# New durations in a list scheduler: the pace of products, and VectorE and GpSimd waiting for each other

## The chip, the cores and the metric

The kernel runs as one program on one core of a Trainium2 chip. The metric is the device time of one execution in microseconds. Before the change it is 1493.85 us, the median of three runs (1490.75 to 1494.23).

Engines are named as in the profile: PE is TensorE, DVE is VectorE, ACT is ScalarE, POOL is GpSimd, and SP is the engine that issues most of the DMAs.

## The reference

256 tokens of 1024 features, with 16 learned meta tokens ahead of them, go through two blocks of two layers each. All is fp32, and each layer is a mixer and a feed-forward part, with norms and residual adds around them:

```python
def first_block(x, meta_tokens, norm_w, ...):        # the meta tokens stand ahead of x
    for i in range(DEPTH):                           # DEPTH = 2
        a_in = rms_norm(hs, norm_w[i, 0])
        mix = gated_deltanet(a_in, ...) if i == 0 else mlstm(a_in, ...)
        hs = hs + keep * rms_norm(mix, norm_w[i, 1])
        f = conv_ffn(rms_norm(hs, norm_w[i, 2]), ...)
        hs = hs + keep * rms_norm(f, norm_w[i, 3])
```

The mixer of the first layer, where most of the kernel's waits lie, is the gated delta rule, in chunks. For each head it needs decay matrices, the products of keys with keys, the inverse of a triangular matrix made from these, and a state that goes from chunk to chunk:

```python
    decay = jnp.exp(jnp.where(incl, G[..., :, None] - G[..., None, :], -jnp.inf))
    a_mat = jnp.eye(CHUNK) + jnp.einsum('bhnid,bhnjd->bhnij', kb, kc) * decay * strict
    sol = lax.linalg.triangular_solve(a_mat, rhs, left_side=True, lower=True)
    ...
    o = rms_norm(o, norm_w) * jax.nn.silu(z)
    return o.reshape(B, L, GDN_VAL_DIM) @ w_out
```

The second block has an even layer (short convolution and sliding-window attention) and an odd layer (gated linear attention and latent attention), each with a SwiGLU feed-forward part. Its mixers and feed-forward parts end in `hs = layer_norm(ALPHA * hs + f)`, where the mean and the variance are taken over the features of a token.

## The kernel before

**Products.** Activations are feature-major: 128 features on the partitions, tokens along the free axis (272 with the meta tokens in the first block, 256 in the second). The weights are streamed once, in 413 chunks of eight tiles of 128 x 128 (`wload`). For each chunk ACT writes the rounded part `wh` (L326) and DVE the remainder `wl` (L327). Each fp32 product is then three matmuls on such parts: `wh` with the high part of the activation, `wh` with its low part, `wl` with its high part (`mm3`, L350 to L352; the same three in `group`, L373, L374 and L376, which works on several products side by side).

**The first mixer** (`gdn`) works in four groups of four heads. A string lists the stages of the groups: projections q, v and z, blocks P, inverses D, token-major values and keys T, states S and outputs O. The parts that matter here:

- Decay matrices, once for all groups: DVE multiplies a mask by the gates (L713, tile `gl_`), PE sums it (L717), ACT takes the exponential (L271) and POOL masks the result (L719, tile `E`).
- Each projection goes through a convolution over tokens: ACT scales, DVE adds three shifted products (L727, tile `kq` or `v`). For the first two projections of group 0 the source is `v_first` in SBUF, otherwise PSUM.
- `gdn_blocks`: products of keys with keys (L810 and L819), then the diagonal blocks of 16 are inverted by substitution on POOL: 15 pairs of a product (L840) and a subtraction (L842), 30 steps. After that POOL takes a power (L843).
- `gdn_inverse`: the inverse is doubled from 16 to 128 by a chain of small products on PE with copies on DVE and ACT between them (L882 is the first, L888 the second).
- `gdn_out`: each output chunk `o` gets its norm: DVE makes the mean square `ss` (L1060 for chunks of 128 tokens), POOL its power (L1064), DVE scales `o` (L1067), PE transposes (L1068), DVE multiplies by the gate (L1071).

The norms of the first block's residuals are made in `post_norm` (a power on POOL at L555).

**The second block's stages** end in `layer_norm`. It works on eight feature tiles m: PE's product, DVE's residual add (L1255 for m < 4, L1259 above), the mean taken out of later and earlier tiles (L1269, L1271), ACT's square, running sums on POOL (L1257, L1263 for the values, L1249 for the squares). Ahead of the last tile's statistics PE sums over the features (`stat_cols`, L422). Where a stage follows, `not_normed` writes high and low parts of the values before the norm is known (ACT L1241, DVE L1242), and PE begins the next stage's products on them (`group`).

**What sets the order.** The kernel is traced as a plain program. Then `IssueOrder` puts each engine's instructions in the order of its queue. It knows the dependencies that the tiles imply, a duration for each instruction (`cost`), the time from the end of an instruction to the start of one on another engine that waits for it (the table HOPS, in `lag`), and a model of TensorE's clock. `search` runs list schedules forwards and backwards in turn, three rounds: `forward` gives starts, `backward` gives due times from the end, and the next `forward` takes the most urgent instruction that is ready. `fix` then writes the order that it finds into the program, as dependencies that need no semaphore. Nothing else follows from the durations: not the instructions, nor their tiles.

Of the kernel before, what the change touches and what calls it, by code (L numbers as in the profile page):

```python
# [13 lines left out]
D = 1024  # L14
# [18 lines left out]
# ---------------------------------------------------------------- host layout  # L33
# [40 lines left out]
# the order of the first mixer: projections q (with k), v and z, products and blocks P, inverses D, token-major values and keys T, states S, outputs O  # L74
# [65 lines left out]
def host(inp):  # L140
# [34 lines left out]
    # second block, even layer: head t of kv 0 beside head 4 + t of kv 1  # L175
# [10 lines left out]
    # odd layer  # L186
# [56 lines left out]
    n = -(-w.shape[0] // CH)  # L243
# [15 lines left out]
# ---------------------------------------------------------------- device  # L259
class Kern:  # L260
# [8 lines left out]
    # ---- helpers  # L269
# [40 lines left out]
    def wload(self, first, need, ahead):  # L310
        """Chunks of weights up to `need`, and `ahead` more as far as the buffers behind `first` go."""
# [27 lines left out]
    def wrow(self):  # L339
        """The next four parts side by side."""  # L340
        ci, j = divmod(self.wpos, CH)
        assert j + 4 <= CH
        for _ in range(4):
            self.wnext()
        return [a[:, j:j + 4].rearrange("p a b -> p (a b)") for a in self.wchunks[ci]]
# [16 lines left out]
    def group(self, items, hook=None):  # L362
        """Several products of K = 8 side by side, so that each part of x serves all of them as it comes."""
# [19 lines left out]
    def halves(self, x, n):  # L383
        """The first four products of K = 16: the last part of x is taken last."""
# [23 lines left out]
    def warm(self, k, ins=None):  # L408
        """Products that nothing reads, behind `ins`, so that the array's clock stays up over a wait."""
# [9 lines left out]
    def stat_cols(self, st, src, n):  # L419
        """Sums over the partitions, one column for each 128 tokens (the last ones overlap)."""  # L420
        for i, s in enumerate(starts(n)):
            r = self.nc.tensor.matmul(st[:, i:i + 1], src[:, s:s + 128], self.ones1, start=True, stop=True)  # L422
        return r

    def bcast(self, out, col, n):
        """A column for each 128 tokens to rows on all partitions."""
# [7 lines left out]
    def row_stat(self, acc, sq, n, warm=0):  # L434
        """Sum of squares over all tiles: the running sum and the last tile."""
# [6 lines left out]
    def acc_sq(self, acc, prev, sq, m):  # L442
        """Running sum of the squares of all tiles but the last."""
# [15 lines left out]
    def rstd(self, st, n, dim, pool, tag="rsy"):  # L459
        """1 / sqrt(st / dim + 1e-6), the same rows on all partitions."""  # L460
# [16 lines left out]
    # ---- norms of the first block  # L477
# [5 lines left out]
    def first_raw(self, pool):  # L483
        """The input of the first mixer, not yet normed, and the columns of its sums of squares."""
# [24 lines left out]
    def pre_norm(self, wname, t0, pool, items, outs, dest=None, st=None, tag="rsy"):  # L509
        """The first products of a stage from its input before the norm, scaled after; then the normed input."""  # L510
# [19 lines left out]
    def post_norm(self, wname, K, x, t0, pool, nxt, tag='mix'):  # L530
        """Output projection, its norm, the residual; then the input of the next stage, not yet normed."""
# [46 lines left out]
    # ---- feed-forward with convolution  # L578
# [38 lines left out]
    # ---- gated delta rule  # L617
    def gdn(self):
# [5 lines left out]
        with ExitStack() as es:  # L624
# [17 lines left out]
            # gates  # L642
# [45 lines left out]
            # cumulative sums and last values  # L688
# [13 lines left out]
            # decay matrices, [j, i]: exponents are the sums of g over j < t <= i  # L702
# [77 lines left out]
    def gdn_blocks(self, g, kq, kq16, E, beta, elg, pool, dpool):  # L780
        """Norms of k, scaled products (attention over E) and the inverses of the diagonal blocks of 16."""
# [9 lines left out]
        # the meta tokens, four heads in slots of 32  # L791
# [3 lines left out]
        # products of keys with keys; the squared norms of the keys on their diagonals  # L795
# [27 lines left out]
        # decayed  # L823
# [3 lines left out]
        # the diagonal blocks of 16, one on a partition  # L827
# [5 lines left out]
        # their inverses by substitution  # L833
# [10 lines left out]
        # products of keys with queries  # L844
# [11 lines left out]
    def gdn_inverse(self, g, X64, Uf, st, pool):  # L856
        """The inverse of the triangular matrix, transposed."""
# [6 lines left out]
        # doubling: blocks of 32, 64 and 128  # L864
# [60 lines left out]
    def gdn_tokens(self, g, kq, v, kq16, v16, st, pool):  # L925
        """Values and keys with the tokens on the partitions, scaled."""
# [29 lines left out]
    def gdn_state(self, g, kq, st, neg, egl, pool):  # L956
        """The states before each chunk; the new values of each chunk take the place of the values."""
# [48 lines left out]
    def gdn_out(self, g, kq, E, st, eg, of, pool):  # L1006
        """The outputs, normed and gated, in place of the gates."""
# [12 lines left out]
        # squared norms of q, one column for each token  # L1020
# [16 lines left out]
        for c in (2, 0, 1):  # L1037
# [16 lines left out]
            # head norm  # L1054
# [21 lines left out]
    # ---- mLSTM  # L1076
# [135 lines left out]
    # ---- second block  # L1212
# [3 lines left out]
    def layer_norm(self, name, K, x, pool, last=False, tags=("xr0", "xr1", "xr2", "xr3")):  # L1216
# [11 lines left out]
        if not last:  # L1228
            # the input of the next stage, not yet normed; beside it the gain and the offset as columns
# [82 lines left out]
    def norm_product(self, i, raw, pool, out=None, scale=1.0):  # L1312
        """A product of an input before the layer norm: without its offset, and the offset; or all of it."""
# [33 lines left out]
    def softmax(self, pool, sbank, tag, scale, mask, sink, vT, out, tp=None):  # L1347
        """sbank: scores [query, (256 keys of block 1 | 128 keys of block 0)], out: [dv, 256 queries]."""
# [81 lines left out]
    def odd(self, xf):  # L1430
# [5 lines left out]
        with tc.tile_pool(name="op", bufs=1, reuse_waits="tile") as pool:  # L1436
# [18 lines left out]
            # gates of the linear attention, rotary key, queries and keys  # L1455
# [22 lines left out]
            # linear attention: decayed products, level by level  # L1478
# [44 lines left out]
            # latent attention: queries, keys, values  # L1523
# [118 lines left out]
    # ---- whole program  # L1642
# [38 lines left out]
# ---------------------------------------------------------------- issue order  # L1681
# [3 lines left out]
# ns from the end of an instruction to the start of one on another engine (or the same) that waits for it  # L1685
# [13 lines left out]
class IssueOrder:  # L1699
    """Orders the traced instructions of each engine: list scheduling, forwards and backwards in turn, over the  # L1700
# [352 lines left out]
```

## Time and profile before

| | |
|---|---|
| time, median of three runs | 1493.85 us (1490.75 to 1494.23) |
| the profiled execution: span | 1496.2 us |
| instructions | 30607 |
| mean granted clock of PE | 0.984 |
| PE busy | 1456.1 us (97%), 12258 matmuls |
| DVE busy | 1056.8 us (71%) |
| ACT busy | 842.9 us (56%) |
| POOL busy | 188.4 us (13%) |
| DMA | 223.96 MB, 150 GB/s on average |
| chain that ended last | PE 86%, DVE 6%, DMA 2%, POOL 2%, issue 2%, ACT 1% |

The profiled execution's own time is its span, 1496.2 us; it is one execution, and 2.35 us above the median of the three timed runs. Times in the rows below are microseconds from the start of this span. A matmul's busy time overlaps with that of the next one, so its pace is read from many of them in a window, and not from the duration of one.

### The profile page before, as it was taken

The numbers are of one execution on the slowest core, as the hardware profiler recorded it, in microseconds if no ns is written. First come the engines' busy times: TensorE is split into PE (matmuls) and PEld (weight loads), VectorE is DVE, ScalarE is ACT, GpSimd is POOL, SyncE is SP. The second block draws the span as 40 slices with busy tenths as digits, with TensorE's granted clock in tenths as the row PEclk, the third lists the DMA queues.
The fourth block names the chain that finished last, engine by engine and source line by source line (L and its number), as shares of the span: only waits on it lengthen the run. The fifth ranks groups of instructions, "written<-read, shape, count | busy, mean of one in ns | idle before, by whom it ended". The sixth has DMA issues, their size and how long they took to land.

```text
span 1496.2 us, 30607 instructions
## 1 busy us (share of the span) xinstructions
PE 1456.1 (97%) x12258; PEld 1403.7 (94%) x12258; DVE 1056.8 (71%) x1976; ACT 842.9 (56%) x1560; POOL 188.4 (13%) x286
## 2 busy tenths in 40 slices
PE   8899999999999999999999999999999999999997
PEld 7898998998999989889999998999999978999997
DVE  8996585548988357657988456686556798875553
ACT  5456565546766446446766446565444666654442
POOL 3472032121000120003000000020001200300011
PEclk9999998999999999999999999989999999999999
DMA  4343422354655534323665543537555424375551
GB/s 161 103 132 103 150 81 62 112 171 147 215 171 180 172 127 157 119 78 119 206 197 179 189 155 113 176 107 222 187 182 183 144 72 155 128 220 188 182 186 57
DMA packets 72670, 223.96 MB, mean 150 GB/s; under 512 B 16784, under 2 KB 18896, under 8 KB 72400
## 3 DMA queue, kind: packets, MB, share of 16 engines
q1 hardware_dynamic: 71952, 220.38, 45.5%
q8 instruction: 96, 1.57, 0.4%
q10 hardware_dynamic: 576, 1.62, 0.3%
q14 instruction: 46, 0.38, 0.1%
HBM read 220.34 MB, written 1.64 MB: 148 GB/s over the span
## 4 chain that ended last, share of the span: by engine, by line
PE 86%; DVE 6%; DMA 2%; POOL 2%; issue 2%; ACT 1%; SPq 0%; DVEq 0%; ACTq 0%; POOLq 0%
PE acc L352 17%; PE acc L350 17%; PE acc L351 17%; PE psa L350 3%; PE psa L352 3%; PE psa L351 3%; PE psb L351 2%; PE psb L352 2%; PE psb L350 2%; PE acc L376 1%; PE acc L373 1%; PE acc L374 1%; DVE wl L327 1%; POOL Xb L842 1%; DVE hs L564 1%
## 5 line engine op out<-in xcount | busy, mean ns | idle before, releaser
L327 DVE TENSOR_TENSOR wl<-wraw,wh 128x1024 fp32r<-128x1024 f32 x413 | 508.1, 1233 | 228.2 <-ACT wh L326 226.8
L326 ACT ACTIVATE wh<-wraw 128x1024 fp32r<-128x1024 f32 x413 | 435.2, 1056 | 277.8 <-PE acc L351 154.9
L352 PE MATMUL acc<-xh,wl 128*128 128x256 f32 (+1 forms) x848 | 246.7, 291 | 1.2 <-DVE wl L327 1.2
L350 PE MATMUL acc<-xh,wh 128*128 128x256 f32 (+1 forms) x848 | 245.5, 290 | 1.0 <-DVE kq L727 1.0
L351 PE MATMUL acc<-xl,wh 128*128 128x256 f32 (+1 forms) x848 | 245.6, 290 | 0.7 <-issue 0.7
L350 PE MATMUL acc<-ah,wh 128*128 128x256 f32 (+1 forms) x704 | 198.0, 283 | 0.0
L351 PE MATMUL acc<-al,wh 128*128 128x256 f32 (+1 forms) x704 | 197.9, 282 | 0.0
L352 PE MATMUL acc<-ah,wl 128*128 128x256 f32 (+1 forms) x704 | 196.7, 282 | 0.0
L352 PEld LDWEIGHTS acc<-xh,wl 128*128 128x128 f32 x848 | 161.5, 191 | 4.3 <-issue 1.7
L350 PEld LDWEIGHTS acc<-xh,wh 128*128 128x128 f32 x848 | 161.3, 190 | 2.4 <-ACT wh L326 1.2
L351 PEld LDWEIGHTS acc<-xl,wh 128*128 128x128 f32 x848 | 161.1, 190 | 1.5 <-issue 0.9
L350 PEld LDWEIGHTS acc<-ah,wh 128*128 128x128 f32 x704 | 132.5, 189 | 0.1
L351 PEld LDWEIGHTS acc<-al,wh 128*128 128x128 f32 x704 | 132.5, 189 | 0.1
L352 PEld LDWEIGHTS acc<-ah,wl 128*128 128x128 f32 x704 | 131.9, 188 | 0.0
L352 PE MATMUL acc<-xnh,wl 128*128 128x272 f32 (+1 forms) x424 | 122.2, 288 | 0.0
L350 PE MATMUL acc<-xnh,wh 128*128 128x272 f32 (+1 forms) x424 | 122.0, 288 | 0.0
L351 PE MATMUL acc<-xnl,wh 128*128 128x272 f32 (+1 forms) x424 | 121.9, 287 | 0.0
L352 PE MATMUL acc<-oh,wl 128*128 128x256 f32 (+2 forms) x304 | 86.4, 286 | 0.5 <-DVE wl L327 0.5
L351 PE MATMUL acc<-ol,wh 128*128 128x256 f32 (+2 forms) x304 | 86.1, 285 | 0.1
L350 PE MATMUL acc<-oh,wh 128*128 128x256 f32 (+2 forms) x304 | 85.2, 286 | 0.0
L350 PEld LDWEIGHTS acc<-xnh,wh 128*128 128x128 f32 x424 | 79.8, 188 | 1.5 <-issue 1.3
L352 PEld LDWEIGHTS acc<-xnh,wl 128*128 128x128 f32 x424 | 79.8, 188 | 1.4 <-issue 1.2
(715 smaller groups left out, 3483.8 us busy)
## 6 DMA issues: line engine op xcount, KB each, us to landing
wraw<-in_w_dram SPq DMA_DIRECT2D x413, 512.0 KB, 3.4
late<-in_late_dram ACTq DMA_DIRECT2D x1, 1206.5 KB, 5.7
hs<-in_x_dram SPq DMA_DIRECT2D x4, 272.0 KB
out_dram<-hs SPq DMA_DIRECT2D x8, 128.0 KB, 1.9
d<-PT SPq DMA_DIRECT2D x32, 9.0 KB, 1.5
cst<-in_cst_dram SPq DMA_DIRECT2D x1, 339.5 KB
A<-d SPq DMA_DIRECT2D x4, 72.0 KB
d<-Xb SPq DMA_DIRECT2D x4, 72.0 KB
```

The lines of the kernel that those rows point to most:

```text
L326: nc.scalar.activation(h, raw, AF.Copy)
L327: nc.vector.tensor_tensor(l, raw, h.bitcast(F32), ALU.subtract)
L350: mm(ps, h, xh, start=start, stop=False)
L351: mm(ps, h, xl, start=False, stop=False)
L352: mm(ps, l, xh, start=False, stop=stop)
L373: mm(o, h, x(k)[0], start=k == 0, stop=False)
L374: mm(o, l, x(k)[0], start=False, stop=False)
L376: mm(o, w[k][0][:, :m], x(k)[1], start=False, stop=k == KD - 1)
L564: V.tensor_tensor(hs, hs, t, ALU.add)
L842: GP.tensor_tensor(Xb[:, j + 1:16, 0:m], Xb[:, j + 1:16, 0:m], tv, sub)
```

## The change

Two durations and one rule change in `IssueOrder`; the rest of the diff takes out comments, and is left out here.

- `cost`: a product matmul of more than 64 output rows on split parts (and a transpose) had N / 2.4 + 2.4 ns for N columns (at least for 256). It now has 0.442 N + 5.5 ns, and at least 112. At 64 output rows or fewer the old formula stays.
- `shares` is new. It marks every tensor-tensor operation and copy of POOL, and each instruction of DVE that reads more than one operand of more than one element a row from SBUF.
- `forward`: a marked instruction doesn't start before the last marked one of the other of these two engines has ended. `backward` is as it was.

```diff
         self.time, self.cols, self.lead = zip(*cost)
+        self.port = [not e and self.shares(k) for k, e in enumerate(self.edge)]
...
+    def shares(self, k):
+        i = self.ins[k]
+        if self.eng[k] == POOL:
+            return str(i.opcode) == "TensorTensor" or str(i.opcode) == "TensorCopy"
+        if self.eng[k] != DVE:
+            return False
+        big = [a for a in i.ins if hasattr(a, "bass_ap") and a.bass_ap.tensor.space != bass.MemoryType.PSUM
+               and row_size([m for _, m in a.ap]) > 1]
+        return len(big) > 1
...
             if ins[0].dtype != F32 or i.is_transpose:
-                return max(n, 256 if m > 64 else 0) / 2.4 + 2.4, n * rows / 128, lead
+                return (max(0.442 * n + 5.5, 112) if m > 64 else n / 2.4 + 2.4), n * rows / 128, lead
...
         last, ticks = -1e3, {}
+        shared, owner = 0.0, DVE
         order, start = [[] for _ in ENGINES], [0.0] * n
...
             d, k = pop(now[e])
             t = max(t, ready[k])
+            if self.port[k] and owner != e:
+                t = max(t, shared)
...
                 free[e] = end = t + self.time[k]
+            if self.port[k]:
+                shared, owner = end, e
             start[k] = t
```

What moves is best seen in the queues. The first place is DVE's queue at the decay matrices of the first mixer. `gl__382`, `gl__405`, `gl__428` and `gl__451` are the masked gates of groups 0 to 3, `v_134` is `v_first`, `kq_474` the convolved queries and keys of group 0. Before:

```order
L713 TENSOR_TENSOR gl__405<-strict_378,gg_346 128x512 x2
L327 TENSOR_TENSOR wl_278<-wraw_275,wh_277 128x1024
L713 TENSOR_TENSOR gl__405<-strict_378,gg_346 128x128
L713 TENSOR_TENSOR gl__428<-strict_378,gg_346 128x512
L727 SCALAR_TENSOR_TENSOR kq_474<-v_134,par_110,kq_474 128x271
L713 TENSOR_TENSOR gl__428<-strict_378,gg_346 128x512
L713 TENSOR_TENSOR gl__428<-strict_378,gg_346 128x128
L713 TENSOR_TENSOR gl__451<-strict_378,gg_346 128x512
L727 SCALAR_TENSOR_TENSOR kq_474<-v_134,par_110,kq_474 128x270
L713 TENSOR_TENSOR gl__451<-strict_378,gg_346 128x512
L727 SCALAR_TENSOR_TENSOR kq_474<-v_134,par_110,kq_474 128x269
L727 SCALAR_TENSOR_TENSOR kq_474<-v_134,par_110,kq_474 128x271
```

After the change, from the second `gl` of group 1 on:

```order
L713 TENSOR_TENSOR gl__405<-strict_378,gg_346 128x512
L727 SCALAR_TENSOR_TENSOR kq_474<-acc_485,par_110,kq_474 128x271
L713 TENSOR_TENSOR gl__405<-strict_378,gg_346 128x128
L696 COPY gc_362<-psb0_367 128x36
L697 TENSOR_TENSOR elg_365<-psb0_367,gc_362 128x36
L713 TENSOR_TENSOR gl__428<-strict_378,gg_346 128x512 x2
L727 SCALAR_TENSOR_TENSOR kq_474<-acc_485,par_110,kq_474 128x270
L713 TENSOR_TENSOR gl__428<-strict_378,gg_346 128x128
L713 TENSOR_TENSOR gl__451<-strict_378,gg_346 128x512 x2
L713 TENSOR_TENSOR gl__451<-strict_378,gg_346 128x128
```

Of the steps that read `v_134`, four (two of 271 elements, two of 270) now stand ahead of the first `gl`, and one of 269 just ahead of the first of these rows; the weight split `wl_278` stands ahead of the first `gl` too. Two steps that read PSUM (`acc_485`) have come in between.

The second place is POOL's queue in the blocks of the last group. L840 and L842 are the substitution steps of that group, and `ss1_3081` is the mean square of an output chunk of the group before it. The difference:

```order
 L840 TENSOR_TENSOR tt1_2832<-A161_2829,Xb1_2831 72x48
 L842 TENSOR_TENSOR Xb1_2831<-Xb1_2831,tt1_2832 72x12x4
+L1064 TENSOR_TENSOR ss1_3081<-ss1_3081,fst_81 128x4
 L840 TENSOR_TENSOR tt1_2832<-A161_2829,Xb1_2831 72x55
 L842 TENSOR_TENSOR Xb1_2831<-Xb1_2831,tt1_2832 72x11x5
@@ -166,5 +168,4 @@
 L842 TENSOR_TENSOR Xb1_2831<-Xb1_2831,tt1_2832 72x4x12
 L840 TENSOR_TENSOR tt1_2832<-A161_2829,Xb1_2831 72x39
-L1064 TENSOR_TENSOR ss1_3081<-ss1_3081,fst_81 128x4
 L842 TENSOR_TENSOR Xb1_2831<-Xb1_2831,tt1_2832 72x3x13
 L840 TENSOR_TENSOR tt1_2832<-A161_2829,Xb1_2831 72x28
```

The power stood behind the 25th substitution step and now stands behind the 8th.

The third place is DVE's queue in the layer norm behind the even layer's mixer. `acc_12152`, `acc_12190` and `acc_12234` are the products of the last three feature tiles, `xr_11948` and `xr_11949` the low parts for the next stage. Before:

```order
L1269 SCALAR_TENSOR_TENSOR hs_76<-hs_76,lnpc_11939 128x256
L1259 TENSOR_TENSOR hs_76<-hs_76,acc_12152 128x256
L1242 SCALAR_TENSOR_TENSOR xr_11948<-hs_76,late_4464,xr_11946 128x256 x4
L327 TENSOR_TENSOR wl_12238<-wraw_12235,wh_12237 128x1024
L1259 TENSOR_TENSOR hs_76<-hs_76,acc_12190 128x256
L1242 SCALAR_TENSOR_TENSOR xr_11949<-hs_76,late_4464,xr_11947 128x256 x2
L327 TENSOR_TENSOR wl_12349<-wraw_12346,wh_12348 128x1024
L1259 TENSOR_TENSOR hs_76<-hs_76,acc_12234 128x256
L1277 TENSOR_SCALAR lnp1_11941<-psb1_11940 128x2
```

After the change:

```order
L1259 TENSOR_TENSOR hs_76<-hs_76,acc_12152 128x256
L1269 SCALAR_TENSOR_TENSOR hs_76<-hs_76,lnpc_11939 128x256
L1242 SCALAR_TENSOR_TENSOR xr_11948<-hs_76,late_4464,xr_11946 128x256
L1259 TENSOR_TENSOR hs_76<-hs_76,acc_12190 128x256
L327 TENSOR_TENSOR wl_12238<-wraw_12235,wh_12237 128x1024
L1242 SCALAR_TENSOR_TENSOR xr_11948<-hs_76,late_4464,xr_11946 128x256
L1259 TENSOR_TENSOR hs_76<-hs_76,acc_12234 128x256
L1242 SCALAR_TENSOR_TENSOR xr_11948<-hs_76,late_4464,xr_11946 128x256 x2
L1277 TENSOR_SCALAR lnp1_11941<-psb1_11940 128x2
```

Three of the four low-part steps and the weight split have moved behind the residual add of `acc_12190`. On PE the sums over the features (L422) stood right behind the last matmul of `acc_12234`; eight matmuls of the next stage's `group` now stand between them.

## Rows read from the trace of the kernel before

**Rows 1.** The page's first part: busy us, share of the span, instructions.

```profile
PE 1456.1 (97%) x12258; PEld 1403.7 (94%) x12258; DVE 1056.8 (71%) x1976; ACT 842.9 (56%) x1560; POOL 188.4 (13%) x286
```

**Rows 2.** Undisturbed windows: length, busy time (and count) by engine, granted clock, DMA share, GB/s.

```profile
440.00:480.00 40.00, 40.00 (x320) 40.00 (x319) 34.07 (x59) 26.75 (x43) 0.00 (x0) 1.00 0.54 176
...
1040.00:1080.00 40.00, 40.00 (x340) 40.00 (x340) 22.46 (x28) 18.99 (x29) 0.00 (x0) 1.00 0.56 186
```

**Rows 3.** Windows with waits, the same columns (PE, PEld, DVE, ACT, POOL).

```profile
0.00:330.00 330.00, 313.96 (x3152) 295.97 (x3153) 234.97 (x535) 186.12 (x419) 99.27 (x195) 0.97 0.38 119
...
540.00:560.00 20.00, 17.27 (x134) 15.96 (x133) 14.24 (x28) 9.55 (x21) 7.22 (x7) 1.00 0.25 85
...
236.50:250.00 13.50, 13.32 (x193) 12.19 (x193) 6.87 (x18) 7.47 (x21) 3.68 (x5) 0.50 0.13 41
...
984.00:994.20 10.20, 10.08 (x47) 10.08 (x48) 6.18 (x13) 2.70 (x5) 1.80 (x3) 0.50 0.61 202
...
1294.60:1298.00 3.40, 3.40 (x18) 3.40 (x17) 3.30 (x8) 0.35 (x1) 0.87 (x1) 0.50 0.47 154
```

**Rows 4.** Lines L713 and L719: ns min/median/max, first and last start; PE's waits.

```profile
L713 DVE TENSOR_TENSOR gl__382<-strict,gg x3: 282/680/683, 29.2 to 30.9; 128x512 f32<-128x512 f32 x2, 128x128 f32<-128x128 f32 x1
...
L713 DVE TENSOR_TENSOR gl__451<-strict,gg x3: 278/1752/1752, 39.2 to 45.0; 128x512 f32<-128x512 f32 x2, 128x128 f32<-128x128 f32 x1
...
  PE psb L717: 3.3, 3
  PE psa L717: 1.6, 2
...
L719 POOL TENSOR_TENSOR E<-E,cst x12: 453/1296/1904, 32.8 to 52.0; 128x512 f32<-128x512 f32 x8, 128x128 f32<-128x128 f32 x4
```

**Rows 5.** DVE's timeline at the decay matrices: start us, us, instruction.

```profile
35.63 1.50 DVE L727 SCALAR_TENSOR_TENSOR kq<-v,par,kq 128x271 f32<-128x271 f32 x1
```

**Rows 6.** Line L840, then timelines of DVE and POOL, 221 to 226 us.

```profile
L840 POOL TENSOR_TENSOR tt<-A,Xb x60: 212/279/1402, 71.4 to 226.4; 72x15 f32<-72x15 f32 x8, 72x28 f32<-72x28 f32 x8, 72x39 f32<-72x39 f32 x8, 72x48 f32<-72x48 f32 x8
...
221.15 0.29 DVE L1060 SCALAR_TENSOR_TENSOR ss<-ss,epq 128x4 f32<-128x4 f32 x1
...
224.27 1.02 POOL L1064 TENSOR_TENSOR ss<-ss,fst 128x4 f32<-128x4 f32 x1
...
225.32 0.87 DVE L1067 TENSOR_SCALAR o<-o,ss 128x128 f32<-128x128 f32 x4 [2.19 <-POOL ss L1064]
```

**Rows 7.** PE's timeline, 224 to 237 us: the instructions that waited, and for what.

```profile
225.75 0.82 PE L1068 MATMUL psb<-fst,o 128*128 128x128 f32 x4 [0.79 <-DVE o L1067]
...
228.56 1.13 PE L1044 MATMUL psb<-S,kq 128*128 128x256 f32 x4 [0.47 <-DVE of L1071]
...
234.28 0.79 PE L882 MATMUL psa<-X,PT 32*32 32x16 f32 x72 [0.87 <-ACT X L877]
...
236.68 0.52 PE L888 MATMUL psa<-Wm,U 32*32 32x16 f32 x24 [0.66 <-DVE Wm L884]
```

**Rows 8.** Timelines of DVE, then PE, at the even mixer's layer norm.

```profile
978.50 3.12 DVE L1242 SCALAR_TENSOR_TENSOR xr<-hs,late,xr 128x256 fp32r<-128x256 f32 x4
...
981.54 1.21 DVE L327 TENSOR_TENSOR wl<-wraw,wh 128x1024 fp32r<-128x1024 f32 x1
982.67 0.41 DVE L1259 TENSOR_TENSOR hs<-hs,acc 128x256 f32<-128x256 f32 x1
...
984.12 1.01 PE L422 MATMUL psb<-ones,lnacc 128*128 128x1 f32 x4 [2.03 <-POOL lnacc L1263]
```

**Rows 9.** PE's timeline at the odd mixer's layer norm.

```profile
1290.87 0.60 PE L422 MATMUL psb<-ones,lnacc 128*128 128x1 f32 x4 [0.62 <-POOL lnacc L1263]
...
1293.15 0.49 PE L422 MATMUL psa<-ones,hs 128*128 128x1 f32 x3 [0.80 <-DVE hs L1259]
```

**Rows 10.** Timelines of POOL and DVE: a power step and a weight split beside it.

```profile
58.34 1.18 POOL L843 TENSOR_TENSOR sn<-nn,cst 128x5 f32<-128x5 f32 x1 [5.07 <-DVE nn L806]
...
58.67 1.19 DVE L327 TENSOR_TENSOR wl<-wraw,wh 128x1024 fp32r<-128x1024 f32 x1
```

## What the change will do to the time, told before it ran

> **What bounds the kernel now.** I read the busy shares first, then windows over the span, then PE's waits and, at each large one, the timelines of the engines it waited for. PE is busy 1456.1 of 1496.2 us [rows 1], and a busy PE is at its pace: where nothing disturbs it, 320 matmuls of 272 columns take 40 us (125.0 ns each) and 340 of 256 columns take 40 us (117.6 ns) [rows 2]. The change removes no matmul, so it can only win back what PE loses: 40.1 us of idle time, and stretches in which the granted clock is 0.5 (1.2 instead of 2.4 GHz). The reader should see in [rows 3] that the clock falls behind some waits and not behind others: it is 0.50 over 236.5 to 250, 984 to 994.2 and 1294.6 to 1298, each right after PE had waited, but 1.00 over 540 to 560, where PE also stood idle 20 - 17.27 = 2.7 us in smaller pieces. A stretch at 0.5 costs half of its length: 6.75, 5.1 and 1.7 us. So the question is whether the new order takes away the waits ahead of these three stretches.
>
> **The change, part by part.** It adds no instruction. Three things in the planner change, and through them the order of all five queues.
>
> *The pace of products.* The old formula gives 272/2.4 + 2.4 = 115.7 ns for a product matmul of 272 columns, the new one 0.442 x 272 + 5.5 = 125.7; for 256 columns 109.1 and 118.7. The trace has 125.0 and 117.6 [rows 2]: the new one is right within 1%. What follows: the first mixer has 1560 product matmuls (counted in the order), so its plan was 1560 x 10 ns = 16 us too short, and each answer of VectorE, ScalarE or POOL came that much earlier, relative to PE, than planned. That slack is now taken out. The Trainium skill (TensorE: Matmul & The Clock Gate, Back-to-back issue gap) speaks against this part: its gap for a single warm matmul is N/2.4 + 2.5 ns, the old formula to 0.1 ns. By it the new pace would be 8% too slow, the work put under each wait 8% too short, and the sum would be that of rival 3; this trace does not bear it out for a stream of products, so I go by the rows.
>
> *The port.* The trace shows the lock. A decay product gl (L713) takes 0.68 us in the median and up to 1.75 while POOL multiplies E (L719, median 1.30) [rows 4]; POOL's substitution products (L840) take a median of 0.28 us and up to 1.40 [rows 6]. One part of the rule is wrong here: the planner also makes VectorE wait for the short power steps of POOL. On the chip a weight split starts 0.33 us into such a step of 1.18 us and takes 1.19 [rows 10], not longer than the 1.21 of another [rows 8]. So I count nothing there. The Trainium skill (SBUF — State Buffer, on the shared port pair) says, as the planner does, that the later of the two waits for the whole instruction; by that this split would have ended 0.85 us later and the sum would gain as much for every power step that the planner moves clear. This row disagrees, so the gain stays out.
>
> *Place 1, decay matrices, 31 to 46 us.* PE waits 3.3 + 1.6 = 4.9 us for gl [rows 4]. Between the first and the last gl VectorE ran four convolution steps that read v from SBUF, so that each of them also met POOL: one of 271 elements took 1.50 us [rows 5], twice the 0.68 of a gl of 512. The new order has three of them ahead of the first gl, the weight split too, and two convolution steps that read PSUM instead. PE gets 24 more product matmuls ahead of this block (24 x 0.125 = 3 us), which cover the later start. The gl still alternate with E, whose 12 products must pass the same port, so part of the wait stays: I take 2.5 us, the middle of the bounds 0 and 4.9.
>
> *Place 2, the last group's blocks, 224 to 250 us.* The scale ss of an output chunk is ready on VectorE at 221.15 + 0.29 = 221.44, but POOL, deep in its substitution, takes its power only at 224.27; VectorE's o waits 2.19 us for it [rows 6], and PE waits 0.79, then 0.47, 0.87 and 0.66 us [rows 7]: 2.8 us, and behind them 13.5 us at half clock [rows 3]. In the new order this power stands behind the 8th of the 30 substitution steps instead of the 25th. The inverse's first products (L882) come 169 product matmuls after this group's key products instead of 151: 18 x 0.125 = 2.3 us more cover against a wait of 0.87. So these waits go and with them the fall of the clock, 6.75 us. Late next: the chain of the inverse, now with 0 to 9 product matmuls between its steps; the waits of 0.87 and 0.66 [rows 7] are such steps, so I put back 1.0 us. Net 8.5 us. Bounds: 2.8 + 6.75 = 9.6 gained, or 2 lost if the power, now ahead of 22 steps, holds the substitution up (22 x 0.1 us, a third of a step's 0.28).
>
> *Place 3, the two layer norms with a next stage, 982 and 1290 us.* At 982.1 PE ends the last product and waits 2.03 us for POOL's sum, which waits for the residual add at 982.67. VectorE did four low-part steps (L1242, 3.12 us) and a weight split (start to start 982.67 - 981.54 = 1.13) ahead of that add [rows 8], whose product had ended 24 matmuls earlier (24 x 0.118 = 2.8 us before 982.1, at 979.3). In the new order one such step stands ahead of the add, so it comes up to 3/4 x 3.12 + 1.13 = 3.5 us earlier, as soon as its product is there, at about 979.4; POOL's sum then ends near 981. PE also does eight raw products first (8 x 0.118 = 0.9 us). I take the whole 2.03 us, and the 5.1 us of half clock behind it: 7.1. At 1290 the same shift takes the waits of 0.62 and 0.80 [rows 9] and 1.7 us of clock: 3.1. Bounds: zero, if another step is late by as much, and these values. Nothing is queued on POOL behind the earlier sum but the next sum.
>
> *Everywhere else.* The feed-forward stages and the tails of the first block's norms move little; PE is covered there. In the first mixer the slack of 16 us is gone, spread over some 85 steps (counted in the order) in which PE waits for another engine. If the planner's hop times were exact this would cost nothing; if all slack had been needed, 16 us. I take 6 us, below the middle, since the port waits that the plan lacked are now counted.
>
> Sum: 2.5 + 8.5 + 7.1 + 3.1 - 6 = 15.2 us less than the profiled execution's span of 1496.2, so 1481.0. That span lies 2.35 us above the median of the runs, 1493.85, so I forecast **1479 us** for the median.
>
> **The rivals.**
> 1. *Only part comes.* Place 2 is a chain of engine changes, and the new order packs the inverse tighter; if the clock falls there as before (it fell behind waits of only 0.47 to 0.87 us), 6.75 us less are gained: 1486. For it: four short waits in a row were enough [rows 7]. Against: the cover grows by 2.3 us. 20%.
> 2. *New waits eat it all.* A list order depends on every small difference. The gains of places 1 and 3 (12.7 us) come, place 2 gives nothing, and the first mixer pays 11 of its 16 us of slack: 1492, no difference. 15%.
> 3. *Slower: the cover is too thin.* The slack of 16 us in the first mixer hid what the planner does not know (when weights land, issue times, what power steps really hold). Without it each of the 85 steps is late, and one more stretch like that at 236.5 goes at half clock (6.75). Against gains of 21.2 this turns the sign from (21.2 - 6.75)/85 = 0.17 us a step; at 0.25 us, about the smallest waits of [rows 7] halved, it gives 21.25 + 6.75 - 21.2 = 6.8 us more: 1501. Against it: [rows 2] show the new pace to be the true one. 15%. The rule on the warm gap from the Trainium skill (the page and section above) would act through this same mechanism; it adds nothing to the chance.
> 4. *The change does not do what it says* cannot hold: the order of PE, VectorE and POOL differs at all three places.
>
> **How the numbers follow.** The forecast case (places 2 and 3 both won) has 50%: from 1469 (all gains at their bounds and nothing lost: 1496.2 - 4.9 - 9.6 - 7.1 - 3.1 - 2.35) to 1484 (the slack costs 11 instead of 6). With rival 1, up to 1488, that is 70%, and rival 2 fills the range to **1469 to 1493**, leaving rival 3 out. A measurement of this kernel tells about 0.3% (4.5 us) from no change. Faster by more than that: forecast and rival 1, 0.70; within: 0.15; slower: 0.15.
>
> **What would show it.** Right: no wait of PE over 1 us at the two layer norms and a granted clock of 1.00 behind them; the power of place 2 within 0.3 us of its scale on VectorE, and no stretch at 0.5 between 220 and 260 us; PE's wait for gl near 2.4 us; PE idle some 30 us instead of 40. Wrong: PE's idle time of the first 330 us above its present 330 - 313.96 = 16.0 us [rows 3], new stretches at 0.5, or the same total with waits at other steps of the first mixer.

## The result and the profile after

The changed kernel takes 1479.65 us (median of 4 runs, 1476.47 to 1482.09), the kernel before 1494.04 us beside it (4 runs, 1490.75 to 1495.3). The ratio is 0.9896 (95% interval 0.9877 to 0.9916): 14.4 us faster, clear of the 0.3% that a measurement can tell. The forecast was 1479 us.

The two profiled executions differ by more, 1496.2 against 1476.0 us of span. An execution's time is 1.77 us above its span here (1477.77 for the span of 1476.0; ahead of the prediction I took the two as equal), so the profile of before was taken on a run some 4 us above its median, and that of after on one 2 us below. What follows compares profiles, so its terms sum to 20.2 us, not to 14.4.

First the granted clock, of before and of after, then the busy shares of after, which answer to [rows 1]:

```profile
core 0: 1496.2 us, clock 0.984
```

```profile
core 0: 1476.0 us, clock 0.995
```

```profile
PE 1442.1 (98%) x12258; PEld 1392.0 (94%) x12258; DVE 1056.2 (72%) x1976; ACT 842.7 (57%) x1560; POOL 194.2 (13%) x286
```

PE's idle time fell from 40.1 to 33.9 us. The clock gave more: the missing share was 0.016 x 1496.2 = 23.9 us and is 0.005 x 1476.0 = 7.4 us, so 16.5 of the 20.2 us. The changed kernel wins by keeping PE at 2.4 GHz, and only a third at most by the waits themselves. The two together are 22.7 us, 2.5 more than the spans differ: less the share that the clock took, PE's busy time grew, from 1456.1 - 23.9 = 1432.2 to 1442.1 - 7.4 = 1434.7 us (estimates from the rows above). Which instructions that comes from no run here shows.

Windows of the changed kernel (columns as in [rows 2]): the last group's blocks (place 2), the end of the first mixer, the two layer norms (place 3), and the odd mixer.

```profile
216.00:260.00 44.00, 43.56 (x546) 40.85 (x545) 30.62 (x71) 27.89 (x82) 16.30 (x38) 1.00 0.33 103
285.00:295.00 10.00, 7.26 (x41) 6.54 (x41) 4.21 (x8) 3.76 (x6) 1.01 (x1) 0.83 0.04 16
969.00:990.00 21.00, 21.00 (x181) 21.00 (x180) 19.52 (x48) 12.49 (x32) 2.81 (x3) 1.00 0.35 106
1275.00:1295.00 20.00, 20.00 (x170) 20.00 (x170) 18.96 (x46) 13.04 (x31) 0.87 (x1) 1.00 0.42 135
1190.00:1210.00 20.00, 14.54 (x95) 11.18 (x94) 18.96 (x47) 13.43 (x31) 0.00 (x0) 0.96 0.23 79
```

The reader should see 1.00 at places 2 and 3, where [rows 3] had 0.50, and a PE that doesn't stop at either layer norm (21.00 of 21, 20.00 of 20). At 285 us, a new place, PE is idle for 2.7 us of 10 and the clock is low in part of it: 0.17 x 10 / 0.5 = 3.4 us at half clock.

To see where the 20 us come from, I took the start of the same product matmul by count (L350 to L352 and L373 to L376 on PE, the same number in both orders) at the borders of the stages:

| up to | after minus before, us | of this stage | forecast |
|---|---|---|---|
| the end of the first mixer (320 us of before) | -7.8 | -7.8 | -5.0 (places 1 and 2, and the slack) |
| the norm behind it (365) | -11.2 | -3.4 | 0 |
| the third norm of the first block (720) | -13.4 | -2.2 | 0 |
| the even mixer (978) | -12.1 | +1.3 | 0 |
| its layer norm (1000) | -19.0 | -6.9 | -7.1 |
| the odd mixer (1285) | -16.5 | +2.5 | 0 |
| its layer norm (1310) | -20.3 | -3.8 | -3.1 |

### The profile page after: what moved, and what is told of

The parts are those of the page before. It is cut to its first block, busy times and chain, and to the rows that moved or that the text cites. A ratio compares the mean times of both kernels' runs of the same rounds, so it can differ in the third digit from the quotient of the medians.

```text
span 1476.0 us, 30575 instructions
## 1 busy us (share of the span) xinstructions
PE 1442.1 (98%) x12258; PEld 1392.0 (94%) x12258; DVE 1056.2 (72%) x1976; ACT 842.7 (57%) x1560; POOL 194.2 (13%) x286
## 4 chain that ended last, share of the span: by engine, by line
PE 84%; DVE 8%; DMA 2%; POOL 2%; ACT 1%; issue 1%; SPq 1%; DVEq 0%; ACTq 0%; POOLq 0%
PE acc L351 17%; PE acc L350 17%; PE acc L352 17%; PE psa L350 3%; PE psa L352 3%; PE psa L351 3%; PE psb L352 2%; PE psb L350 2%; PE psb L351 2%; DVE wl L327 2%; PE acc L376 2%; PE acc L373 1%; PE acc L374 1%; POOL Xb L842 1%; POOL tt L840 1%
## 5 line engine op out<-in xcount | busy, mean ns | idle before, releaser
L350 PE MATMUL acc<-xh,wh 128*128 128x256 f32 (+1 forms) x848 | 244.8, 289 | 2.1 <-DVE kq L727 2.1
L352 PE MATMUL acc<-xh,wl 128*128 128x256 f32 (+1 forms) x848 | 245.0, 289 | 1.4 <-DVE wl L327 1.4
L350 PE MATMUL acc<-ah,wh 128*128 128x256 f32 (+1 forms) x704 | 197.1, 282 | 0.0
L352 PE MATMUL acc<-ah,wl 128*128 128x256 f32 (+1 forms) x704 | 196.5, 282 | 0.0
L350 PEld LDWEIGHTS acc<-xh,wh 128*128 128x128 f32 x848 | 159.7, 188 | 5.1 <-issue 1.9
L352 PEld LDWEIGHTS acc<-xh,wl 128*128 128x128 f32 x848 | 160.1, 189 | 3.4 <-DVE wl L327 2.1
L350 PEld LDWEIGHTS acc<-ah,wh 128*128 128x128 f32 x704 | 132.3, 189 | 0.1
L352 PEld LDWEIGHTS acc<-ah,wl 128*128 128x128 f32 x704 | 131.8, 188 | 0.1
L350 PE MATMUL acc<-xnh,wh 128*128 128x272 f32 (+1 forms) x424 | 122.1, 288 | 0.0
L352 PE MATMUL acc<-xnh,wl 128*128 128x272 f32 (+1 forms) x424 | 122.0, 288 | 0.0
L350 PE MATMUL acc<-oh,wh 128*128 128x256 f32 (+2 forms) x304 | 86.0, 288 | 1.5 <-ACT oh L474 1.5
L352 PE MATMUL acc<-oh,wl 128*128 128x256 f32 (+2 forms) x304 | 87.1, 289 | 0.0
L350 PEld LDWEIGHTS acc<-xnh,wh 128*128 128x128 f32 x424 | 79.8, 188 | 1.8 <-issue 1.3
L351 PEld LDWEIGHTS acc<-xnl,wh 128*128 128x128 f32 x424 | 80.0, 189 | 0.9 <-issue 0.8
```

The lines of the kernel that those rows point to most:

```text
L350: mm(ps, h, xh, start=start, stop=False)
L351: mm(ps, h, xl, start=False, stop=False)
L352: mm(ps, l, xh, start=False, stop=stop)
```

## The experiments

Each kernel was timed beside the kernel before on the same chip (4 to 10 runs); the medians of before, from 11 to 15 runs, lay at 1493.3 to 1495.2 us. A line of three dots marks what is left out of a listing.

**The two parts apart.** First the pace without the port, in the kernel before:

```diff
-                return max(n, 256 if m > 64 else 0) / 2.4 + 2.4, n * rows / 128, lead
+                return (max(0.442 * n + 5.5, 112) if m > 64 else n / 2.4 + 2.4), n * rows / 128, lead
```

> Only the new pace of products, no rule on the port. Theory (the gain sits at the named waits, and the port rule moves the instructions there): in this plan the residual add at the even layer norm still stands behind four low-part steps, and the power of place 2 behind 26 of the 30 substitution steps, so those waits and the half clock behind them stay; 1487 to 1496 us. Rival (right durations of PE are what counts): most of the 14 us gained, 1484 us or less.

Measured: 1506.14 us, ratio 1.0076 (1.0048 to 1.0104), 11 us slower than before. Neither theory had this (the prediction's third rival did). The profile shows where it happens. These are the timelines of POOL, ACT and PE at the third inverse of the first mixer, then a window behind it, then two rows of PE's waits (us in total, times, longest), and last two steps of the same substitution on POOL in the kernel before:

```profile
120.33 1.34 POOL L840 TENSOR_TENSOR tt<-A,Xb 72x48 f32<-72x48 f32 x1
...
123.08 1.47 POOL L842 TENSOR_TENSOR Xb<-Xb,tt 72x28 f32<-72x28 f32 x1
...
130.86 0.72 ACT L877 ACTIVATE X<-X,cst 128x144 f32<-128x144 f32 x2 [5.47 <-DMA X<-d]
...
131.32 1.14 PE L882 MATMUL psa<-X,PT 32*32 32x16 f32 x66 [2.87 <-ACT X L877]
134.06 1.16 PE L888 MATMUL psa<-Wm,U 32*32 32x16 f32 x72 [1.59 <-DVE Wm L884]
```

```profile
131.50:138.00 6.50, 4.91 (x152) 3.98 (x147) 5.75 (x11) 4.67 (x10) 1.42 (x2) 0.51 0.26 88
```

```profile
PE st L939 <- POOL v L937: 3.3, 2, 2.6
...
PE st L810 <- POOL kq L793: 1.7, 1, 1.7
```

```profile
115.94 1.33 POOL L840 TENSOR_TENSOR tt<-A,Xb 72x55 f32<-72x55 f32 x1
...
119.09 1.18 POOL L840 TENSOR_TENSOR tt<-A,Xb 72x28 f32<-72x28 f32 x1
```

Two substitution steps that take about 0.25 us beside nothing take 1.34 and 1.47, their result goes through memory, ACT gets it at 130.86, PE waits 2.87 and 1.59 us, and the clock is down to 0.51 behind it. But the kernel before has steps as long in this substitution, and PE waits for nothing there: between 100 and 170 us its profile lists no wait of PE. So POOL is late in both, and what the pace alone takes away is the work that covered it: from the start of this substitution to the inverse's first products the traces have 127 product matmuls on PE, against 150 before and 147 in the changed kernel (23 x 0.125 = 2.9 us, as much as PE waits). Over the whole run PE waits 10.9 us for POOL (the POOL rows of that view added up), against 6.2 before and 2.3 in the changed kernel. By the same count of products the first mixer ends 8.0 us later than before, and 6.0 of this arise between 60 and 200 us. Then the port without the pace, that is the changed kernel with the old formula put back in that line:

> Only the rule on the port, with the old pace. Theory: the residual add stands behind one low-part step as in the changed kernel, so place 3 is won (10 us), and the power of place 2 stands behind about the 14th step; decay matrices as before. 1478 to 1486 us, no stretch at half clock at the two layer norms. Rival (pace counts): 1490 us or more.

Measured: 1485.37 us, ratio 0.9942 (0.9925 to 0.9958). The theory holds: both layer norms at a clock of 1.00, with short waits left. The third window is place 2, and the clock does not fall there either. In this kernel the power stands behind the 15th substitution step and starts at 222.36 us, 0.1 us after its scale is ready:

```profile
970.00:992.00 22.00, 20.41 (x171) 19.99 (x170) 17.21 (x46) 13.74 (x29) 7.26 (x6) 1.00 0.22 73
1275.00:1300.00 25.00, 23.10 (x196) 22.90 (x195) 21.11 (x52) 17.11 (x41) 7.71 (x9) 1.00 0.24 75
225.00:262.00 37.00, 35.81 (x478) 32.82 (x477) 24.40 (x55) 23.34 (x69) 11.09 (x21) 1.00 0.30 93
```

So the parts don't add: +11 and -10 us alone, -14 together.

**Places 3 and 2 by hand.** These kernels keep the plan of before and move single instructions in its finished order, so that nothing else differs. The first moves VectorE's residual adds:

```diff
...
+        move(DVE, reads(DVE, "acc_12190")[0], outs(DVE, "xr_11948")[1])
+        move(DVE, reads(DVE, "acc_12234")[0], outs(DVE, "xr_11948")[-1])
+        move(DVE, reads(DVE, "acc_15893")[0], outs(DVE, "xr_15651")[1])
+        move(DVE, reads(DVE, "acc_15937")[0], outs(DVE, "xr_15651")[-1])
...
```

(`move(e, k, behind)` puts instruction k of engine e behind another; `outs` and `reads` find those that write or read a tile.)

> The plan of before, and in its finished order only VectorE's residual adds at the two layer norms moved ahead of low-part steps and weight splits. Theory: 7.1 + 3.1 = 10.2 us less than before, 1484 us, no half clock behind 982 and 1290. Rival (the wait is taken over by the next late step, or the clock falls anyway): 1491 us or more, with the stretch at 0.5 still there.

Measured: 1491.3 us (10 runs), ratio 0.9975 (0.9961 to 0.9988), 3.9 us less. That is 7 us short of the theory, and in number where the rival had it. PE's timeline at the two layer norms, then a window behind each:

```profile
981.39 0.61 PE L422 MATMUL psb<-ones,lnacc 128*128 128x1 f32 x4 [0.33 <-POOL lnacc L1249]
...
1283.19 0.61 PE L422 MATMUL psb<-ones,lnacc 128*128 128x1 f32 x4 [0.60 <-POOL lnacc L1263]
```

```profile
984.00:994.00 10.00, 9.54 (x80) 9.32 (x78) 9.67 (x28) 6.09 (x14) 0.87 (x1) 1.00 0.62 197
...
1283.00:1289.50 6.50, 6.26 (x37) 5.98 (x38) 6.40 (x16) 1.88 (x4) 1.88 (x3) 0.74 0.44 156
```

At the first the mechanism is shown: the wait falls from 2.03 [rows 8] to 0.33 us, no stretch at half clock follows, and by the count of products this norm gains 5.5 us in the profile. At the second the wait of 0.60 us stays and with it the half clock, as long as before (0.26 x 6.5 / 0.5 = 3.4 us, 3.4 in [rows 3]); only the wait of 0.80 [rows 9] is gone, and the gain is about 1. PE's order, in which the changed kernel puts products of the next stage ahead of the sums, is left as it was here. The second kernel moves POOL's power:

```diff
...
+        step = [k for k in outs(POOL, "Xb1_2831") if str(o.ins[k].opcode) == "TensorTensor"][3]
+        move(POOL, [k for k in outs(POOL, "ss1_3081")][-1], step)
...
```

(Here `outs(POOL, "Xb1_2831")` counts subtractions alone, so `[3]` is the 8th of the 30 steps.)

> The plan of before, and in its finished order only POOL's power at place 2 moved from behind the 25th to behind the 8th substitution step. Theory: the waits of 0.79 and 0.47 us go, but those of 0.87 and 0.66 at the inverse stay, as PE's order is unchanged; if two short waits are not enough for the clock to fall, 1.3 + 6.75 = 8 us less, 1486 us; if they are, 1 us less, 1493 us. Rival (the power holds the substitution up): 1 to 2 us more, 1495 us.

Measured: 1498.91 us, ratio 1.0032 (1.0017 to 1.0048): 3.7 us slower, the rival. POOL's timeline, then PE's:

```profile
221.14 1.02 POOL L1064 TENSOR_TENSOR ss<-ss,fst 128x4 f32<-128x4 f32 x1 [5.38 <-DVE ss L1060]
222.13 0.28 POOL L840 TENSOR_TENSOR tt<-A,Xb 72x55 f32<-72x55 f32 x1
...
232.72 0.33 PE L939 MATMUL st<-fst,v 128*128 128x128 f32 x1 [4.93 <-POOL v L937]
```

POOL comes to the power 5.38 us before its scale is there, and stands. The 22 steps behind it are late by up to 6 us, the copy behind them (L937) by 4.6, and PE waits 4.93 us for the copy.

**The power steps.** The prediction held that a power step doesn't hold the port, against the planner:

```diff
+            if str(i.opcode) == "TensorTensor" and len(i.outs[0].ap) == 2 and row_size([m for _, m in i.outs[0].ap]) <= 16:
+                return False
             return str(i.opcode) == "TensorTensor" or str(i.opcode) == "TensorCopy"
```

> The changed kernel, but POOL's short power steps (16 elements or fewer) are not marked as users of the port. Theory (a weight split beside a power step takes its usual 1.19 us, so the mark wins nothing): within 3 us of the changed kernel, 1477 to 1483 us. Rival (the later one waits out the whole power step, so that the plan needs the mark): some twenty power steps of 0.5 to 1.5 us get VectorE work beside them, 1485 us or more.

Measured: 1473.99 us (1472.55 to 1475.23), ratio 0.9862 (0.9841 to 0.9883). The mark doesn't help, as said, and it even costs: this kernel is 5.7 us below the changed one's median, more than the theory allowed. Its windows at the end of the first mixer and in the odd mixer show 1.00, where the changed kernel's clock fell (0.83 and 0.96 above):

```profile
280.00:290.00 10.00, 9.38 (x70) 8.79 (x70) 5.34 (x10) 4.17 (x12) 1.86 (x1) 1.00 0.31 107
1185.00:1210.00 25.00, 22.81 (x159) 17.56 (x158) 24.51 (x68) 17.69 (x42) 0.00 (x0) 1.00 0.21 64
```

**Is it luck?** A list order can turn on any small difference. So every hop time was made 3 ns longer, which means nothing, in three of the kernels:

```diff
-        return HOPS.get((self.eng[a], self.eng[b]), 120)
+        return HOPS.get((self.eng[a], self.eng[b]), 120) + 3
```

The changed kernel:

> The changed kernel, with every hop time of the planner 3 ns longer: a change with no meaning, which shuffles the list order. Theory (the gain follows from the right durations and would be found by any such plan): 1476 to 1485 us. Rival (the gain is the luck of one list order): more than 6 us away from the changed kernel, 1486 us or more, or 1474 or less.

Measured: 1477.47 us, ratio 0.9889 (0.9863 to 0.9916). The kernel without marked power steps:

> The kernel without marked power steps, with every hop time 3 ns longer. Theory (the mark of the power steps costs something, since it makes the planner wait where the chip doesn't): near the unshuffled one, 1471 to 1477 us. Rival (its 5 us over the changed kernel were the luck of one order): 1478 us or more.

Measured: 1471.63 us (1470.63 to 1475.07), ratio 0.9858 (0.9837 to 0.988), the fastest of all. The pace alone:

> The new pace without the port rule, with every hop time 3 ns longer. Theory (the right pace alone takes away the slack that hid POOL's lateness at the port): again slower than before, 1497 to 1510 us. Rival (its 11 us were the luck of one order): 1490 us or less.

Measured: 1508.58 us, ratio 1.0109 (1.0083 to 1.0135). Each shuffled kernel lies within 2.5 us of its own kind, and the kinds are 1472 to 1474, 1477 to 1480 and 1506 to 1509 us: the differences between the kinds come from the durations, and not from one lucky order each, as far as two orders of a kind can tell. The kernel before was not shuffled: what its 1494 us owe to the luck of its order is not shown. The granted clock of the fastest, and its PE:

```profile
core 0: 1470.0 us, clock 0.998
```

```profile
PE 1439.5 (98%) x12258; PEld 1389.1 (94%) x12258; DVE 1056.8 (72%) x1976; ACT 841.9 (57%) x1560; POOL 193.0 (13%) x286
```

**Which part of the program.** The new durations for the first mixer's instructions only (`k < self.cut`, where `cut` is the number of instructions traced up to its end), then for those behind it only:

> The new durations for the first mixer's instructions alone, the old ones behind it. Theory from the two traces (the first mixer's norm comes 7.8 us earlier in the changed kernel, the rest gains 12.8): the order at the even layer norm is that of before, so its wait and half clock stay; 1485 to 1489 us. Rival (one part carries all): 1481 or less, or 1493 or more.

> The old durations for the first mixer, the new ones for everything behind it. Theory: the layer norms come out as in the changed kernel (no wait over 0.5 us, no half clock there), the first mixer keeps its waits; 1481 to 1486 us, and with the run before it the two gains add up to that of the changed kernel within 3 us. Rival (the parts interact, so that each alone gives little): 1489 us or more.

Measured: 1487.08 us, ratio 0.9959 (0.994 to 0.9978), and 1487.14 us, ratio 0.9951 (0.9934 to 0.9968). The sum, 6.3 + 6.2 = 12.5 us, is that of the changed kernel (14.4) within the 3 us. The second lies 1 us above what was expected of it. The window of the first layer norm in the first kernel (the wait and the low clock are there), and in the second (gone):

```profile
970.00:992.00 22.00, 20.09 (x139) 19.47 (x139) 17.58 (x42) 13.13 (x33) 2.58 (x3) 0.84 0.30 98
```

```profile
970.00:992.00 22.00, 22.00 (x189) 22.00 (x188) 20.00 (x49) 16.11 (x37) 8.22 (x8) 1.00 0.24 82
```

**Which engine's lateness.** In `forward`, the pace and one side of the rule:

```diff
-            if self.port[k] and owner != e:
+            if self.port[k] and owner != e and e == POOL:
```

> The new pace, and in the planner only POOL waits for VectorE at the port, VectorE never for POOL. Theory (what the pace alone lacked is that POOL is late: its substitution steps take 0.28 us alone and up to 1.40 beside VectorE): most of the gain, 1476 to 1486 us. Rival (it is VectorE's lateness, as at the decay matrices): 1492 us or more.

Measured: 1486.34 us, ratio 0.9949 (0.993 to 0.9967). And with `e == DVE`:

> The new pace, and in the planner only VectorE waits for POOL, POOL never for VectorE. Theory: little of the gain behind the first two hundred microseconds, 1492 to 1506 us. Rival (VectorE's lateness counts): 1476 to 1486 us.

Measured: 1500.97 us, ratio 1.0056 (1.0032 to 1.0081). Beside the pace alone at 1506.14, POOL's side takes off some 20 us, VectorE's alone about 5, both together some 27. The 5 are hardly clear of the scatter: single runs lie at 1496 to 1507 us with VectorE's side, and at 1501 to 1509 without it. The first kernel lands 0.3 us above the expected range. In the second, PE's largest wait is still for POOL:

```profile
PE st L810 <- POOL kq L793: 5.1, 3, 2.8
```

## Why the prediction was right, and where it was not

**The frame** held: PE is at its pace, so only waits and clock can be won, and three stretches at half clock were named. All three are gone (0.50 in [rows 3], 1.00 now). But five more stood in the trace of before that were not costed, at 11, 45, 346, 1216 and 1493 us. Those at 45 and 346 are gone too, the one at 1216 is half as long, and a new one stands at 290. So the norm behind the first mixer gained 3.4 us without a term, 1.7 of them by the stretch at 346. Two windows of before, then one of after at that norm:

```profile
1216.10:1222.90 6.80, 6.28 (x16) 4.29 (x16) 6.61 (x13) 3.97 (x10) 0.00 (x0) 0.50 0.42 137
...
345.70:349.10 3.40, 3.40 (x13) 2.92 (x13) 1.36 (x4) 2.02 (x4) 0.00 (x0) 0.50 0.02 5
...
332.00:352.00 20.00, 18.74 (x141) 17.97 (x139) 19.25 (x37) 13.35 (x25) 3.23 (x4) 1.00 0.50 177
```

The odd mixer, also without a term, pays 2.5 us back: in the window from 1190 us above, PE is idle for 5.5 of 20.

**Place 1**, -2.5 us: too small, some -4.8 came. The last product of the block starts 45.76 us into the span before, and 43.21 now, but 24 more product matmuls (3 us) now stand ahead of it, so those 2.5 us are not the gain. The window from the block on, before and after:

```profile
28.00:60.00 32.00, 26.38 (x192) 24.79 (x191) 30.39 (x60) 16.47 (x33) 17.01 (x15) 0.95 0.25 80
...
28.00:60.00 32.00, 29.49 (x235) 28.44 (x234) 31.87 (x74) 18.31 (x39) 18.27 (x15) 1.00 0.36 116
```

PE's idle time falls by 3.1 us, and the stretch at half clock behind the block, which had no term, is gone: 1.7. I had half of the wait for gl stay; none is left, and the block starts 3 us later instead, with a new wait of 1.0 us for ScalarE (`egl`). The row that answers to the second of [rows 4]:

```profile
L713 DVE TENSOR_TENSOR gl__451<-strict,gg x3: 540/939/1754, 39.2 to 41.8; 128x512 f32<-128x512 f32 x2, 128x128 f32<-128x128 f32 x1
```

Its median fell from 1.75 to 0.94 us; one step still meets POOL (1.75).

**Place 2**, -8.5 us: right in size, wrong in its cause. The step that failed is "In the new order this power stands behind the 8th of the 30 substitution steps instead of the 25th. ... So these waits go". Timelines of DVE, POOL and PE of after:

```profile
217.87 0.17 DVE L1060 SCALAR_TENSOR_TENSOR ss<-ss,epq 128x4 f32<-128x4 f32 x1 [0.27 <-ACT sq L1058]
...
220.79 1.01 POOL L1064 TENSOR_TENSOR ss<-ss,fst 128x4 f32<-128x4 f32 x1
...
238.50 0.79 PE L882 MATMUL psa<-X,PT 32*32 32x16 f32 x72 [0.25 <-ACT X L877]
...
241.23 0.79 PE L888 MATMUL psa<-Wm,U 32*32 32x16 f32 x72 [0.17 <-DVE Wm L884]
```

The scale is ready at 218.04 and its power starts 2.75 us later, as long as before (224.27 - 221.44 = 2.83). Moved alone, the power costs 3.7 us, because POOL then stands before it. The trace of before could have told: its 8th step ends at 216.01, 5.4 us before the scale is ready at 221.44 (POOL's timeline of before):

```profile
215.73 0.28 POOL L842 TENSOR_TENSOR Xb<-Xb,tt 72x48 f32<-72x48 f32 x1
```

What the run shows instead is that the whole plan moved: the substitution starts 4.1 us later (217.15 against 213.09) and the scale is ready 3.4 us earlier, so that the same row of POOL's queue fits, and PE has 115 product matmuls from there to the inverse's first products, 86 before. The port rule alone, with the power behind the 15th step and 117 products, has no half clock there either, so the 8th place is not what does it. The other half of the step, more cover ahead of the inverse, fits these counts, but no run moves it by itself. The waits of 0.87 and 0.66 are 0.25 and 0.17, and with the two at the output chunk gone this is 2.4 us and the clock's 6.75, 9.1.

**Place 3**, -7.1 and -3.1 us: 6.9 and 3.8 by the table, and shown alone for the first norm, where the move by hand took the wait and the low clock away (it brought 3.9 us by the medians, both norms together). Timelines of DVE and PE of after, which answer to [rows 8]:

```profile
967.17 0.42 DVE L1259 TENSOR_TENSOR hs<-hs,acc 128x256 f32<-128x256 f32 x1 [0.53 <-PE acc L352]
...
970.78 0.95 PE L422 MATMUL psb<-ones,lnacc 128*128 128x1 f32 x8
```

The add waits for its product now, and PE's sums for nothing.

**The lost slack**, +6 us: near 7. Up to 28 us PE's idle time falls by 1.0 us (4.4 to 3.4); with 4.8 at place 1 and 9.1 at place 2 that is 14.9, and the first mixer stands at -7.8. What is paid back was forecast over some 85 steps, but more than half of it is at one place, the mixer's end (PE's timeline of after, then the 50 us around it before and after):

```profile
286.59 0.82 PE L1068 MATMUL psb<-fst,o 128*128 128x128 f32 x4 [1.09 <-DVE o L1067]
...
288.94 0.64 PE L350 MATMUL acc<-oh,wh 128*128 128x272 f32 x3 [1.53 <-ACT oh L474]
```

```profile
280.00:330.00 50.00, 49.38 (x390) 48.76 (x389) 26.19 (x34) 26.46 (x54) 8.81 (x8) 1.00 0.47 157
...
272.00:322.00 50.00, 47.24 (x357) 46.22 (x356) 25.28 (x33) 25.47 (x53) 9.92 (x8) 0.97 0.43 136
```

That is 2.1 us of idle time and 1.7 by the 3.4 us at half clock. Between places 1 and 2 PE's idle time grows by 0.8. The other 2.5 us or so are as much as PE's busy time grew over the whole run; that the two are the same is not shown.

**The rivals.** The first two did not come: no half clock is left at place 2. The third, the cover too thin, is what the pace alone does: 11 to 15 us slower than before. It does not happen here because the port rule puts POOL's lateness into the plan, as "the port waits that the plan lacked are now counted" put it. I gave it 15%, charged the pace 6 us and gave the port rule no term of its own for paying this back; in fact the pace alone costs 11 to 15 us, and the rule more than pays for it. The power steps were judged rightly: the row of one weight split beside one power step [rows 10] foretold the runs without the mark.

**The signs.** At the two layer norms and from 220 to 260 us the signs of being right came as named. The power within 0.3 us of its scale (2.75), a wait of 2.4 us for gl (none) and an idle time of PE of some 30 us (33.9) did not. One sign of being wrong came too, the new stretch at half clock at 290 us; PE's idle time of the first 330 us did not rise (13.9 us, 16.0 before).

**How close it was** is in part luck. The forecast is the median of before, 1493.85, less the sum of 15.2, and the medians differ by 14.4. But the terms were read from one profile, and the two profiles differ by 20.2: the sum was 5 us short of them. That the profile of before lay 4 us above its median and that of after 2 us below gives 6 us back.

## What to carry to other kernels

A planner that is too optimistic about one engine can be kept alive by being too optimistic about another: correct one duration alone and the hidden error can come out (+11 us here), so correct them together, and check each part in a run of its own. Shuffle the plan with a change that means nothing before you believe a small difference. And in an in-order queue a step is worth moving forward only if its input is there: moved by hand it blocked what stood behind it.

## What the hardware showed that I had not expected

- A power of two to five elements on POOL takes 0.7 to 1.2 us and does not keep VectorE off: in the profiles of before and after 12 weight splits start inside a power step, and each took 1.19 to 1.23 us, the median of all splits being 1.22. The other way round the power waits: one of three elements that starts 0.16 us into a split took 1.78 us, one beside nothing 0.85 (timelines of after, DVE and POOL, then POOL):

```profile
324.57 1.23 DVE L327 TENSOR_TENSOR wl<-wraw,wh 128x1024 fp32r<-128x1024 f32 x1
324.73 1.78 POOL L555 TENSOR_TENSOR rsv<-rsv,fst 128x3 f32<-128x3 f32 x1 [6.49 <-DVE rsv L554]
...
677.28 0.85 POOL L555 TENSOR_TENSOR rsv<-rsv,fst 128x3 f32<-128x3 f32 x1 [2.81 <-DVE rsv L554]
```

  The plan that marks these steps both ways is 5 to 6 us slower than the one that marks them in neither (1479.65 and 1477.47 against 1473.99 and 1471.63 us); a plan in which only the power waits was not run.
- The granted clock varies from run to run of the same program: over 15 runs of the kernel before it was 0.983 to 0.989, and the time 1497.48 to 1491.56 us. Such a scatter of 6 us is as large as many of the terms here, and one profile is one draw from it.
- The clock doesn't follow the idle time alone. In the kernel before PE was idle for 2.7 us of 20 between 540 and 560 us at a clock of 1.00 [rows 3]; with the new durations in the first mixer alone it was idle for 1.9 of 22 between 970 and 992 us (20.09 busy), and the mean clock was 0.84. Which pattern of waits makes it fall is left open.
